# First projection of a hybrid encoder block: two value groups visited once for rows 2 to 8, the other four once for rows 4 to 8

## Chip, core and metric

The kernel runs on one NeuronCore of a Trainium2 chip. The metric is the device time of one execution in microseconds. The kernel before was run three times: 1234.67 us median, 1233.9 to 1236.42.

## The reference

One layer on 256 tokens of width 2048, all in float32. A modulation `mod = silu(c) @ w_ada + b_ada` gives six vectors of 2048 (shift, scale and gate, for each of two halves). Then:

```
h    = rms_norm(x, norm1_w) * (1 + scale1) + shift1
proj = h @ w_in                     # mq mk mv mo (gates) dq dk dv, 6152 columns
h_ml = mLSTM in chunks of 64 (conv and silu on mq, mk; values mv; output gate sigmoid(mo))
o_da = differential attention (q, k normed and rotated; two softmax maps a head; values dv)
x    = x + gate1 * (concat(h_ml, o_da) @ w_out)
h    = rms_norm(x, norm2_w) * (1 + scale2) + shift2
g, u = split(h @ w_gate_up)
x    = x + gate2 * ((silu(g) * u) @ w_down)
```

## The kernel before

**Products.** A float32 matrix product is made of three products of rounded parts: weights and activations are each split into a high part (ScalarE, `wh`, `hh`) and a low rest (VectorE, `wl`, `hl`), and TensorE adds high x high, high x low and low x high. One *step* (a "tick" in the code) is 256 rows of one group of 512 output columns: 12 matmuls of 128x512, two column halves of the activations' tokens, three products each. `weights_hi` and `weights_lo` split the weights up to two steps ahead of their use, four buffers of each. A *visit* is a run of steps of one output group that adds up in PSUM. When a visit ends, `project_done` copies the sum to `proj` (first visit of the group) or adds it there (VectorE, 128x1024).

**First projection.** `w_in` has twelve groups of 512 columns, each with eight steps (the list's rows 0 to 8, each 256 of the 2048 rows of the contraction). `EARLY` are two groups of q, two of k of the attention, and mq and mk; `LATE` are `DV` (two attention value groups), `MV` (two mLSTM value groups) and `MO` (two output gate groups). `SWEEPS` (line 52) lists in which order the groups are visited and for which rows. Sweep rows p0 to p1 need the transposed, modulated and split activations `h0_p0` to `h0_(p1-1)` (`make_hT`, line 447). The first 24 steps visit every group for row 0, then for row 1.

**Modulation.** The vectors of `w_ada` are made tile by tile (192 tiles of 512 KB), in the fixed order of `items` (line 300): for p = 0 to 7 four tiles of scale1 and four of shift1, then the 32 tiles of gate1, then scale2 and shift2, then gate2. The tiles of scale1 with p = 0, 1, 3, 4, 6, 7, of shift1 with p under 4 and of gate1 are multiplied on TensorE (`gv`, line 216 in the profile), the others on VectorE (line 185, `ada<-ada,silc`). `h0_p` needs the eight tiles of its p. The tiles share four buffers (`NADA`): the code issues a new tile's transfer when one has been used, on the SyncE queue, which also issues the weights' transfers (three buffers of 1 MB).

**Order of the work.** All engines' queues are written out by a plan in Python. For each step i the main loop (line 1338) splits weights, then calls `ada_use` until the number that `due(i)` names is reached, then runs works that are ready (`plan.run`; it holds them back while its account of VectorE's or ScalarE's backlog is over 2.3), then `ada_idle`, which uses a tile ahead of time if the plan takes it for landed and its engine for free, then forces whatever the step needs (`plan.until`), and then writes the 12 matmuls. Every engine works its queue in order. `due` (line 1249) comes from `ADA_PLAN` (line 1397): each entry (sweep, tiles, margin) spreads so many tiles evenly over the steps of that sweep, less the margin at its end, on top of 8:

```
a, b = spans[span]
loads.append((a, max(b - margin, a + 1), n))
...
n += k * min(max(i + 1 - a, 0), b - a) / (b - a)
```

**After the projection.** `prep` (norm, rotation, transposes of q, k), `conv`, `attend`, `attend_values`, `ml_scores`, `ml_values` and the rest are put between the steps as soon as the visits they need (`in{g}_8`) are done. The output projection starts at step 96 with the attention half.

Of the kernel before, what the change touches and what calls it, by code (L numbers as in the profile page):

```python
# [37 lines left out]
def on_pe(s, p):  # L38
# [9 lines left out]
DQ, DK, DV, MQ, MK, MV, MO = (0, 1), (2, 3), (4, 5), 6, 7, (8, 9), (10, 11)  # L48
EARLY = (DQ[0], DK[0], MQ, MK, DQ[1], DK[1])
LATE = (DV[0], DV[1], MV[0], MV[1], MO[0], MO[1])  # L50
FILL = 2
SWEEPS = (
    (EARLY + LATE, 0, 1), (EARLY + LATE, 1, 2), (EARLY + LATE, 2, 4), (LATE[6 - FILL:], 4, 6),
    (EARLY, 4, 8), (LATE[:6 - FILL], 4, 8), (LATE[6 - FILL:], 6, 8),
)
SQ0, SQ1 = True, False
FPAIRS = 6
# [107 lines left out]
def tile_block(ctx, tc, x, c, pos, par, w_ada, w_in, w_gt, w_out, w_gu, w_dn, out):  # L165
# [1076 lines left out]
    def load(span, n, margin):  # L1242
        a, b = spans[span]
        loads.append((a, max(b - margin, a + 1), n))

    for key, n, margin in ADA_PLAN:
        load(key, n, margin)
# [146 lines left out]
        return next(self.gen)  # L1394


ADA_PLAN = ((0, 12, 3), (1, 16, 4), (2, 24, 3), (3, 4, 0), (4, 8, 0), (5, 8, 0), ("wo", 16, 22), ("f0", 24, 5), ("f1", 32, 5), ("f2", 32, 8))


def _layout(a):  # L1400
# [68 lines left out]
```

## Time and profile before

| what | value |
|---|---|
| median of 3 runs | 1234.67 us |
| profiled execution, its own time | 1233.24 us |
| its span, first to last instruction | 1231.5 us |
| granted TensorE clock, mean | 0.992 |
| TensorE busy | 1208.9 us, 98% |
| VectorE busy | 815.3 us, 66% |
| ScalarE busy | 587.1 us, 48% |
| first projection, steps 0 to 95 | from 29.10 to 391.72 us |
| its third sweep, steps 24 to 47 | from 123.14 to 196.07 us |
| HBM traffic | 254 GB/s over the span |

In the profile, PE is TensorE, DVE VectorE, ACT ScalarE, POOL GpSimd, SPq the SyncE queue that issues transfers. Rows of the time line give start, duration, engine, line, operation, what is written and read, and how many were merged. Rows of waits give the engine and line that waited, what it waited for, and then total, number and longest. Rows of a window give its length, the busy time of each engine, the granted clock, the share of time that the DMA engines were busy, and GB/s. A matmul's busy time (0.39 us) overlaps the next one's: their starts are 0.227 us apart, so a step without other work takes 2.72 us.

### The profile page before, as it was taken

To read this page: it belongs to the slowest core of one execution; us is meant where nothing else is said; L and a number is where in the kernel's file an instruction comes from. 1 tells how busy PE (TensorE), PEld (TensorE's weight loads), DVE (VectorE), ACT (ScalarE), POOL (GpSimd) and SP (SyncE) were. 2 spreads that over 40 slices of the span, in tenths; PEclk is the share of its full clock that TensorE was granted. 3 is DMA by queue.
4 is the path that set the end of the run, shared out by engine and by line. 5 is a ranking of instruction groups with operands and counts; after the bars stand their busy time and mean duration, and the time that the engine had idled before them with its cause. 6 is when DMAs were issued, how large, how long until landed. Compare 5 with 4: busy or idle time off the path is not lost.

```text
span 1231.5 us, 15419 instructions
## 1 busy us (share of the span) xinstructions
PE 1208.9 (98%) x5842; PEld 956.2 (78%) x5842; DVE 815.3 (66%) x1064; ACT 587.1 (48%) x817; POOL 113.2 (9%) x250
## 2 busy tenths in 40 slices
PE   6999999999999999999999999999999999999998
PEld 2667878666778787788888888888888878888886
DVE  2656977577587998887988977445455454545443
ACT  3654454457566645855434544444444443343342
POOL 1010121210212412101100000000000000000000
PEclk8999999999999999999999999999999999999999
DMA  8879898757676898798999756555545545646471
GB/s 335 303 279 372 327 372 293 294 187 292 206 288 233 320 358 336 265 345 305 350 342 334 274 195 221 200 177 196 184 177 199 201 171 171 222 171 232 160 256 52
DMA packets 63260, 313.84 MB, mean 255 GB/s; under 512 B 6993, under 2 KB 7377, under 8 KB 41169
## 3 DMA queue, kind: packets, MB, share of 16 engines
q1 hardware_dynamic: 63186, 312.86, 70.1%
q8 instruction: 46, 0.75, 0.2%
q14 instruction: 28, 0.23, 0.1%
HBM read 310.73 MB, written 2.10 MB: 254 GB/s over the span
## 4 chain that ended last, share of the span: by engine, by line
PE 96%; DMA 1%; DVE 1%; ACT 1%; issue 0%; SPq 0%; POOL 0%; ACTq 0%
PE gv L216 3%; PE acc('dn', 0)_8036 L571 2%; PE acc('dn', 0)_8036 L569 2%; PE acc('dn', 2)_8838 L571 2%; PE acc('dn', 2)_8838 L570 2%; PE acc('dn', 1)_8458 L571 2%; PE acc('dn', 1)_8458 L570 2%; PE acc('dn', 0)_8036 L570 2%; PE acc('dn', 1)_8458 L569 2%; PE acc('dn', 2)_8838 L569 2%; DMA ada<-in_w_ada_dram 1%; PE apart('dn', 3)_9219 L571 1%; PE apart('dn', 3)_9219 L570 1%; PE acc('dn', 3)_9218 L571 1%; PE acc('dn', 3)_9218 L570 1%; PE apart('dn', 3)_9219 L569 1%
## 5 line engine op out<-in xcount | busy, mean ns | idle before, releaser
L181 DVE TENSOR_TENSOR wl<-r,wh 128x1024 fp32r<-128x1024 f32 x392 | 474.5, 1222 | 254.3 <-ACT wh L211 252.8
L211 ACT ACTIVATE wh<-r 128x1024 fp32r<-128x1024 f32 x392 | 410.3, 1058 | 409.6 <-DMA r<-in_w_gu_dram 62.1
L185 DVE SCALAR_TENSOR_TENSOR ada<-ada,silc 128x1024 f32<-128x1024 f32 x120 | 144.8, 1219 | 0.0
L377 POOL TENSOR_TENSOR modc<-part,gsum 128x2 f32<-128x2 f32 (+1 forms) x34 | 25.4, 747 | 395.1 <-DVE ada L185 277.5
L216 PE MATMUL gv<-ada,early 128*32 128x256 f32 x576 | 46.3, 416 | 4.3 <-DMA ada<-in_w_ada_dram 4.2
L216 PEld LDWEIGHTS gv<-ada,early 128*32 128x32 f32 x576 | 13.4, 112 | 29.4 <-issue 20.0
L569 PE MATMUL acc('dn', 0)_8036<-wh,aTh 128*128 128x512 f32 x88 | 35.9, 408 | 0.0
L379 POOL TENSOR_TENSOR modc<-modc,gsum 128x2 f32<-128x2 f32 (+1 forms) x58 | 30.9, 533 | 46.8 <-DVE ada L185 43.4
L571 PE MATMUL acc('dn', 0)_8036<-wh,aTl 128*128 128x512 f32 x88 | 34.3, 390 | 0.0
L570 PE MATMUL acc('dn', 0)_8036<-wl,aTh 128*128 128x512 f32 x88 | 34.3, 389 | 0.0
L569 PE MATMUL acc('dn', 1)_8458<-wh,aTh 128*128 128x512 f32 x88 | 34.2, 389 | 0.0
L570 PE MATMUL acc('dn', 1)_8458<-wl,aTh 128*128 128x512 f32 x88 | 34.2, 389 | 0.0
L571 PE MATMUL acc('dn', 1)_8458<-wh,aTl 128*128 128x512 f32 x88 | 34.2, 389 | 0.0
L569 PE MATMUL acc('dn', 2)_8838<-wh,aTh 128*128 128x512 f32 x88 | 34.2, 389 | 0.0
L570 PE MATMUL acc('dn', 2)_8838<-wl,aTh 128*128 128x512 f32 x88 | 34.2, 389 | 0.0
L571 PE MATMUL acc('dn', 2)_8838<-wh,aTl 128*128 128x512 f32 x88 | 34.2, 389 | 0.0
L181 DVE TENSOR_TENSOR hl<-hx,hh 128x512 fp32r<-128x512 f32 (+1 forms) x18 | 11.4, 632 | 26.5 <-ACT hh L211 26.2
L211 ACT ACTIVATE hx<-pt,modc,gcol 128x256 f32<-128x256 f32 (+1 forms) x36 | 17.4, 534 | 17.3 <-PE pt L220 11.5
L211 ACT ACTIVATE gr<-gv 128x256 f32<-128x256 f32 x18 | 6.9, 383 | 32.6 <-PE gv L216 32.6
L570 PEld LDWEIGHTS acc('dn', 0)_8036<-wl,aTh 128*128 128x128 f32 x88 | 16.5, 188 | 4.2 <-issue 1.0
L569 PEld LDWEIGHTS acc('dn', 0)_8036<-wh,aTh 128*128 128x128 f32 x88 | 16.5, 188 | 4.2 <-issue 1.0
L211 ACT ACTIVATE aTh<-at 128x512 fp32r<-128x512 f32 x22 | 11.9, 595 | 15.9 <-PE at L220 15.9
(987 smaller groups left out, 3019.0 us busy)
## 6 DMA issues: line engine op xcount, KB each, us to landing
ada<-in_w_ada_dram SPq DMA_DIRECT2D x192, 512.0 KB, 5.7
r<-in_w_gu_dram SPq DMA_DIRECT2D x76, 1024.0 KB, 5.0
r<-in_w_dn_dram SPq DMA_DIRECT2D x44, 1024.0 KB, 4.8
r<-in_w_in_dram SPq DMA_DIRECT2D x36, 1024.0 KB, 6.9
r<-in_w_out_dram SPq DMA_DIRECT2D x16, 1024.0 KB, 7.4
r<-in_w_in_dram SPq DMA_DIRECT2D x24, 512.0 KB, 5.9
r<-in_w_gu_dram SPq DMA_DIRECT2D x24, 512.0 KB, 5.3
x<-in_x_dram SPq DMA_DIRECT2D x4, 512.0 KB, 5.6
```

The costliest lines, as they stand in the source:

```text
L181: nc.vector.tensor_tensor(o, a, b, op=op)
L185: nc.vector.scalar_tensor_tensor(out=o, in0=a, scalar=s, in1=b, op0=op0, op1=op1, accum_out=accum)
L211: nc.scalar.activation(o, a, func, **kw)
L216: nc.tensor.matmul(o, l, r, start=start, stop=stop, **kw)
L377: nc.gpsimd.tensor_tensor(o, parts[0], parts[1], op=ALU.add)
L379: nc.gpsimd.tensor_tensor(o, o, y, op=ALU.add)
L569: nc.tensor.matmul(o, ah[:, s], wh[:, r], start=t["start"] and j == 0, stop=False)
L570: nc.tensor.matmul(o, ah[:, s], wl[:, r], start=False, stop=False)
L571: nc.tensor.matmul(o, al[:, s], wh[:, r], start=False, stop=t["stop"] and j == 1)
```

## The change

The third sweep (rows 2 to 4) leaves out the two attention value groups; `FIRST` = 2 names them. The extra visits of the two output gate groups (rows 4 to 6, ahead of the fourth sweep, and rows 6 to 8 at the end) are gone. The fourth sweep (q, k, mq, mk for rows 4 to 8) follows the third at once. After it the two attention value groups are visited once for rows 2 to 8, six steps each, and the other four late groups once for rows 4 to 8. There are 46 visits in place of 50, and 96 steps as before. Step 24 to 35 visit the same groups and rows in both. `ADA_PLAN` has its entries for the third to sixth sweep set anew: 28, 8, 4 and 4 tiles with no margin, in place of 24 (margin 3), 4, 8 and 8.

```
-FILL = 2
+FIRST = 2
 SWEEPS = (
-    (EARLY + LATE, 0, 1), (EARLY + LATE, 1, 2), (EARLY + LATE, 2, 4), (LATE[6 - FILL:], 4, 6),
-    (EARLY, 4, 8), (LATE[:6 - FILL], 4, 8), (LATE[6 - FILL:], 6, 8),
+    (EARLY + LATE, 0, 1), (EARLY + LATE, 1, 2), (EARLY + LATE[FIRST:], 2, 4), (EARLY, 4, 8),
+    (LATE[:FIRST], 2, 8), (LATE[FIRST:], 4, 8),
 )
...
-ADA_PLAN = ((0, 12, 3), (1, 16, 4), (2, 24, 3), (3, 4, 0), (4, 8, 0), (5, 8, 0), ("wo", 16, 22), ("f0", 24, 5), ("f1", 32, 5), ("f2", 32, 8))
+ADA_PLAN = ((0, 12, 3), (1, 16, 4), (2, 28, 0), (3, 8, 0), (4, 4, 0), (5, 4, 0), ("wo", 16, 22), ("f0", 24, 5), ("f1", 32, 5), ("f2", 32, 8))
```

## The prediction

> **What bounds the kernel now.** I read the page first (busy shares, then the 40 slices), then who waited for whom, then the third sweep of the first projection in windows and in order of time.
>
> ```profile
> span 1231.5 us, 15419 instructions
> ...
> PE 1208.9 (98%) x5842; PEld 956.2 (78%) x5842; DVE 815.3 (66%) x1064; ACT 587.1 (48%) x817; POOL 113.2 (9%) x250
> ...
> PE   6999999999999999999999999999999999999998
> ...
> DVE  2656977577587998887988977445455454545443
> ```
>
> TensorE is at work in every slice after the first, so no removed VectorE or ScalarE work shortens the span by itself. The time can only move by TensorE waits. Here are all that it has after 75 us:
>
> ```profile
> PE acc('gu', 0, 0)_4441 L569 <- ACT hh L211: 2.3, 2, 1.1
> PE acc('wo', 0)_3635 L571 <- DVE odl L185: 0.7, 1, 0.7
> PE pt L220 <- DVE hx L190: 0.7, 1, 0.7
> ```
>
> The reader is to see how little there is to win: only the 0.7 us at the start of the output projection lies behind the changed sweeps. The other two belong to the turn from output projection to feed-forward, which the change leaves alone. So the question is what the change may cost, and that is read from the third sweep (steps 24 to 47 before, 123.14 to 196.07 us):
>
> ```profile
> core 0: us, PE busy (x) PEld busy (x) DVE busy (x) ACT busy (x) POOL busy (x), PEclk, DMA share, GB/s
> 123.14:196.07 72.93, 72.93 (x369) 56.57 (x369) 61.37 (x70) 33.20 (x43) 14.38 (x22) 1.00 0.91 342
> 126.19:161.39 35.20, 35.20 (x178) 27.53 (x178) 35.06 (x43) 15.69 (x19) 8.17 (x10) 1.00 0.96 360
> 145.00:165.00 20.00, 20.00 (x112) 14.68 (x110) 16.58 (x20) 8.88 (x12) 3.49 (x4) 1.00 1.00 384
> ```
>
> For 35 us in it VectorE is as full as TensorE (35.06 of 35.20), and in part of that the DMA engines are full too (share 1.00 at 384 GB/s). TensorE does not wait there, but only just:
>
> ```profile
> 126.19 1.21 DVE L185 SCALAR_TENSOR_TENSOR ada<-ada,silc 128x1024 f32<-128x1024 f32 x1
> ...
> 127.33 1.21 DVE L185 SCALAR_TENSOR_TENSOR ada<-ada,silc 128x1024 f32<-128x1024 f32 x1
> ...
> 144.72 1.22 DVE L185 SCALAR_TENSOR_TENSOR ada<-ada,silc 128x1024 f32<-128x1024 f32 x1
> ...
> 149.28 1.22 DVE L181 TENSOR_TENSOR wl<-r,wh 128x1024 fp32r<-128x1024 f32 x1
> ```
>
> ```profile
> 148.13 0.39 PE L569 MATMUL acc('in', 1, 2)_1314<-wh,hh 128*128 128x512 f32 x1
> ...
> 150.85 0.39 PE L569 MATMUL acc('in', 3, 2)_1356<-wh,hh 128*128 128x512 f32 x1
> ```
>
> Step 33 starts at 148.13 and step 34 at 150.85, 2.72 us apart. Step 34's low weight half (wl) is ready at 149.28 + 1.22 = 150.50, 0.35 us ahead. VectorE's large operations follow each other in 127.33 - 126.19 = 1.14 us.
>
> **What the change removes.** Four visits, so four VectorE additions of an accumulator to proj, 4 x 1.14 = 4.6 us. They are hidden: the waits above hold none on proj. The count of matmuls (96 steps of 12), weight bytes and transfers (24 of 512 KB, 36 of 1024 KB) stay. I count 0.
>
> **What it moves.** The second half of the rows (h0_4 to h0_7) is now wanted from step 44, one group per step, so h0_7 by step 47 instead of 55. The plan therefore takes adaLN tiles 36 to 63 in 20 steps, 1.4 a step, where it took 24 in 21, 1.14 a step. I number tiles by their issue from 0: 44 to 47 and 52 to 55 go to VectorE, 48 to 51 and 56 to 59 to TensorE. By the plan's formula 48 and 49 are due at step 33 (now 35 and 36), 52 at 36 (38), 56 at 38 (42), 60 to 63 at 41 to 43 (48 to 51). The four ring buffers let a tile be issued only when the one four before it has been used.
>
> ```profile
> 145.97 0.33 SPq L316 DMA_DIRECT2D ada<-in_w_ada_dram  x1
> ```
>
> ```profile
> ada<-in_w_ada_dram SPq DMA_DIRECT2D x1, 512.0 KB, 5.0
> ```
>
> ```profile
> 153.67 0.64 PE L216 MATMUL gv<-ada,early 128*32 128x256 f32 x8
> ...
> 176.29 0.64 PE L216 MATMUL gv<-ada,early 128*32 128x256 f32 x8
> ```
>
> ```profile
> DMA to landing us min/median/max: 3.8/5.6/8.2
> ```
>
> **First new wait: tiles 48 and 49 at step 33.** Now tile 44's product starts at 144.72, tile 48 is issued at 145.97 when it is done, lands 5.0 us later (150.97) and is read at 153.67, 2.7 us to spare. After the change VectorE has 15 operations ahead of tile 44 from 126.19 on, not 16; at (144.72 - 126.19)/16 = 1.16 us it starts at 143.6 and ends at 144.7. Tile 45 is two operations on, ending at 147.0; tile 49 is issued then and with the median 5.6 us lands at 152.7. But TensorE comes to the pair in front of step 33, at about 148.1, and to tile 49 0.5 us later: it waits 152.7 - 148.6 = 4.1 us in all (2.3 with the shortest landing, 6.7 with the longest). Behind it on TensorE stand all matmuls of the sweep. The late wl halves (under 1 us by the same count) disappear under it. I take 4.0.
>
> **Second: tile 56 at step 38.** Now its predecessor 52 is due at step 38:
>
> ```profile
> 164.96 0.48 PE L569 MATMUL acc('in', 5, 2)_1476<-wh,hh 128*128 128x512 f32 x1
> ```
>
> ```profile
> 165.94 1.22 DVE L185 SCALAR_TENSOR_TENSOR ada<-ada,silc 128x1024 f32<-128x1024 f32 x1
> ```
>
> Its product ends at 167.16, 2.2 us after step 38 began, and only then can 56 be issued. After, 52 is due at 36 and 56 at 38, two steps or 5.44 us on. 2.2 + 5.6 - 5.44 = 2.4 us of wait; with 3.8 and 8.2 us, 0.6 and 5.0. I take 2.0, because a sweep that has just waited leaves the DMA engines less behind. Tiles 50, 51 and 57 to 63 come out with room by the same count.
>
> **The clock after a wait.** One long wait of this kind is in the trace, at step 9:
>
> ```profile
> PE gt L216 <- ACT hh L211: 2.3, 1, 2.3
> PE acc('in', 0, 0)_305 L570 <- DVE wl L181: 0.5, 1, 0.5
> PE gt L216 <- DVE hl L181: 0.4, 1, 0.4
> ```
>
> ```profile
> 64.90:67.50 2.60, 0.36 (x2) 0.00 (x0) 0.00 (x1) 2.54 (x5) 0.54 (x3) 1.00 0.98 384
> 68.00:71.40 3.40, 3.15 (x13) 1.97 (x17) 1.64 (x3) 0.27 (x1) 0.00 (x0) 0.64 0.75 252
> 72.50:79.00 6.50, 6.50 (x40) 4.37 (x38) 2.45 (x2) 2.84 (x4) 0.00 (x0) 1.00 0.70 236
> ```
>
> After 2.3 + 0.4 us of waiting the granted clock was 0.64 over 3.4 us, a loss of 0.36 x 3.4 = 1.2 us. The first new wait is longer than that, so I add 1.2; the second is shorter, 0 (both bounds: 0 to 1.2 each). [...] The trace's 2.7 us sufficed, and I go by it.
>
> **Small terms.** h0_7's transposes and splits come about a step before step 47 (the plan holds works back while VectorE's account is over 2.3): 0.4 us, from 0 to the 2.7 us that the forced one at step 9 cost. The value sums end 4 to 6 steps sooner, so odl is in time: -0.7 (0 to -1.0). TensorE's small matvecs cost less in pairs than alone:
>
> ```profile
> 214.88 1.07 PE L216 MATMUL gv<-ada,early 128*32 128x256 f32 x16
> 220.64 0.64 PE L216 MATMUL gv<-ada,early 128*32 128x256 f32 x8
> ```
>
> 2 x 0.64 - 1.07 = 0.2 us for each pair; 50 and 51, a pair now, come apart: 0.3, and up to 1.5 either way for the 32 tiles of the gate, which the plan puts where it finds room.
>
> **Sum**: 4.0 + 2.0 + 1.2 + 0.4 - 0.7 + 0.3 = +7.2 us on the profiled execution's own 1233.24 (span 1231.5 and 1.7 around it): 1240.4, or 1240.5. That execution lies 1.4 us under the median of the runs (1234.67), inside or just under their 1233.9 to 1236.42; against the median it is +0.5%. Within 0.2%, or 2.5 us, no change could be told.
>
> **Rivals.** (a) *The transfers are in time.* With landings near 3.8 us the waits are 2.3 and 0.6, the clock holds, h0_7 is free and the start of the output projection gives 0.7: +2.2 us, and with luck in pairing +0.7: 1234 to 1236, no change. For it: over 160 to 170 us the queue already served more than the 384 quoted, and landings vary twofold. Against: the shortest landing is not the usual one while the engines are full.
> (b) *Faster.* The place is the start of the output projection: attention and cells done 4 to 6 steps earlier give back 0.7 to 1.0 us, and gate tiles in pairs 1.5; it decides if tiles 48, 49 and 56 are there when asked for, that is, if the landing is under some 2 us for 49. -2.5: 1230.7. Against: no landing under 3.8 us in that stretch.
> (c) *DMA becomes the bound of the whole sweep.* 20 weight halves and 28 tiles are 48 x 0.524 = 25.2 MB; at 384 GB/s 65.5 us, where TensorE needs 20 x 2.72 + 7.6 (72.93 - 24 x 2.72, its small work) = 62.0. 3.5 us of that, the two waits at 4.1 and 2.4, both with 1.2 of clock, and a forced h0_7 (2.7): +15, 1248. For it: 25.2 MB in 62 us is 406 GB/s. Against: six weight steps lie in the buffers when the sweep starts.
> (d) *The change doesn't do what it says*: if the plan's idle rule took tiles ahead of the due count, rates would stay; but it did so for two of 24 only. In (a).
>
> **Chances.** Forecast 0.53, (a) 0.25, (b) 0.08, (c) 0.14. The forecast's own range is 1237 to 1245.5. For 8 of 10 I leave out most of (b) and the far end of (c): 1233 to 1247.5. Faster by over 0.2%: 0.08, (b). Within: 0.25, (a). Slower: 0.67.
>
> **What would show it.** Idle time of TensorE in front of gv at steps 33 and 38, put down to the ada transfer, 4 and 2 us, right if there, wrong if gv follows its matmul without a gap. A granted clock under 1 for about 3.4 us after the first. No odl wait at the output projection. VectorE full from 126 to 150 us and 4 fewer proj additions. The prediction is wrong if the third sweep has no TensorE wait: then the time is that of (a) or (b).

## The result, and the profile after

The changed kernel takes 1249.18 us (median of 4 runs, 1247.71 to 1250.11); the kernel before, beside it, 1234.29 (4 runs, 1233.35 to 1236.42). The ratio is 1.0118, with a 95% interval of 1.0106 to 1.0130. The change makes the kernel 14.9 us slower. The prediction had the sign and half of the size.

The page of the changed kernel, profiled in an execution of 1248.64 us:

```profile
span 1246.9 us, 15415 instructions
...
PE 1214.1 (97%) x5842; PEld 957.1 (77%) x5842; DVE 810.9 (65%) x1060; ACT 586.0 (47%) x817; POOL 105.4 (8%) x250
```

TensorE has the same 5842 instructions, VectorE 4 fewer and 4.4 us less work (815.3 to 810.9): the four additions are gone, and the time rose all the same. So waits or the clock of TensorE must hold the loss. All waits of TensorE after 75 us (engine, line, what it waited for; total, times, longest):

```profile
PE gv L216 <- DMA ada<-in_w_ada_dram: 4.2, 3, 2.3
PE pt L220 <- DVE hx L190: 2.7, 1, 2.7
PE acc('gu', 0, 0)_4433 L569 <- ACT hh L211: 2.1, 2, 1.1
PE acc('in', 0, 4)_1662 L569 <- ACT hh L211: 1.8, 1, 1.8
PE at L220 <- DVE fp L181: 1.8, 2, 1.4
PE ot L220 <- ACT ml L211: 0.7, 1, 0.7
PE acc('gu', 1, 5)_5856 L570 <- DVE wl L181: 0.4, 1, 0.4
```

Seven groups where there were three, 13.7 us in place of 3.7. The first, fourth and sixth lie in the first projection; the second, third, fifth and seventh lie in stages that the change doesn't touch. To see how much time each place took, I read the start of the first matmul of a step from the order of time, in both traces. The difference in length of each stretch, after less before (and the same for three experiments below):

| steps | before, us | changed kernel | before, tiles at the new rate | changed, slower tiles | changed, old places | changed, both |
|---|---|---|---|---|---|---|
| up to 0 | 29.10 | +0.37 | +0.67 | +0.39 | +0.54 | +0.67 |
| 0 to 24 | 94.04 | -0.76 | -0.41 | +0.47 | -0.47 | -0.72 |
| 24 to 33 | 24.99 | +4.43 | +4.65 | 0.00 | +3.87 | 0.00 |
| 33 to 38 | 16.83 | +0.62 | +0.85 | 0.00 | +0.88 | +0.17 |
| 38 to 48 | 31.11 | +7.06 | +3.50 | +7.74 | +7.02 | +8.92 |
| 48 to 104 | 225.80 | -4.10 | +7.85 | -3.65 | -4.13 | -3.66 |
| 104 to 126 | 59.84 | 0.00 | +4.47 | 0.00 | 0.00 | 0.00 |
| 126 to 130 (the turn) | 15.58 | +4.47 | +2.79 | +0.03 | +1.57 | +0.01 |
| 130 to 188 | 160.84 | -0.01 | -0.04 | +0.99 | 0.00 | -0.01 |
| 188 to 224 (end of gate and up) | 102.61 | +3.33 | +0.25 | +3.03 | +0.62 | +0.06 |
| 224 to the end | 470.79 | -0.02 | -0.01 | -0.02 | -0.01 | +0.03 |

(48 to 104 gives time back because the transposes for `h0_7` and the small products behind them, which stood at steps 52 and 53, now stand at steps 46 and 47.) Not every microsecond of a profile is the edit's: two runs below are the kernel before, unchanged up to step 104, and they reach that step 1.17 and 1.00 us later than it. Up to step 104 the sum is +7.6 us, beside the predicted +7.2. Another 7.8 us comes later: 4.5 at the turn from output projection to feed-forward, 3.3 in the last feed-forward sweep of gate and up. These the prediction did not see.

The third sweep of the changed kernel in the order of time (start, duration, and in brackets the idle time ahead and what ended it):

```profile
150.36 0.64 PE L216 MATMUL gv<-ada,early 128*32 128x256 f32 x8 [2.26 <-DMA ada<-in_w_ada_dram]
151.61 0.64 PE L216 MATMUL gv<-ada,early 128*32 128x256 f32 x8 [0.61 <-DMA ada<-in_w_ada_dram]
...
169.05 0.64 PE L216 MATMUL gv<-ada,early 128*32 128x256 f32 x8 [1.38 <-DMA ada<-in_w_ada_dram]
...
201.68 0.50 PE L569 MATMUL acc('in', 0, 4)_1662<-wh,hh 128*128 128x512 f32 x1 [1.83 <-ACT hh L211]
```

Tiles 48 and 49 are waited for in front of step 33, tile 56 in front of step 38, and `h0_7`, forced late, in front of step 47. The SyncE queue shows tile 48's issue, and then 56's:

```profile
144.13 3.75 SPq L316 DMA_DIRECT2D ada<-in_w_ada_dram  x3
...
164.67 3.76 SPq L316 DMA_DIRECT2D ada<-in_w_ada_dram  x3
```

From 144.13 to the use at 150.36 are 6.2 us, from 164.67 to 169.05 4.4 us: TensorE stands idle for what is left of these two landings.

The turn, first in the kernel before and then in the changed one:

```profile
487.97 0.70 PE L220 MATMUL pt<-ident,hx 128*128 128x128 f32 x4 [0.65 <-DVE hx L190]
489.81 0.50 PE L569 MATMUL acc('gu', 0, 0)_4441<-wh,hh 128*128 128x512 f32 x1 [1.15 <-ACT hh L211]
```

```profile
497.67 1.11 PE L220 MATMUL pt<-ident,hx 128*128 128x128 f32 x4 [2.73 <-DVE hx L190]
499.76 0.80 PE L569 MATMUL acc('gu', 0, 0)_4433<-wh,hh 128*128 128x512 f32 x1 [0.98 <-ACT hh L211]
```

The transposes wait 2.1 us longer, and the matmul behind them takes 0.80 us in place of 0.50: the granted clock is 0.50 from 497.66 to 504.49 us. ScalarE ahead of it in the changed kernel:

```profile
475.73 0.63 ACT L211 ACTIVATE junk<-x2r 128x512 bf16<-128x512 f32 x1 [4.18 <-DVE x2r L181]
...
490.97 2.01 ACT L211 ACTIVATE wh<-r 128x1024 fp32r<-128x1024 f32 x2 [5.81 <-DMA r<-in_w_gu_dram]
```

And the issue of the first feed-forward weights, before and after:

```profile
471.52 0.33 SPq L515 DMA_DIRECT2D r<-in_w_gu_dram  x1
```

```profile
478.00 4.43 SPq L316 DMA_DIRECT2D ada<-in_w_ada_dram  x2
482.52 1.11 SPq L515 DMA_DIRECT2D r<-in_w_gu_dram  x1
```

A shift by the 7.6 us so far would give 479.1; it is issued 3.4 us later than that, behind two tile issues in the same queue (478.00 + 4.43), which wait for VectorE's products. ScalarE's high halves then wait 5.81 us for these weights.

### The profile page after: what moved, and what is told of

Its sections match the earlier page's. It is cut to its first block, busy times and chain, and to the rows that moved or that the text cites. A ratio compares the mean times of both kernels' runs of the same rounds, so it can differ in the third digit from the quotient of the medians.

```text
span 1246.9 us, 15415 instructions
## 1 busy us (share of the span) xinstructions
PE 1214.1 (97%) x5842; PEld 957.1 (77%) x5842; DVE 810.9 (65%) x1060; ACT 586.0 (47%) x817; POOL 105.4 (8%) x250
## 4 chain that ended last, share of the span: by engine, by line
PE 85%; DVE 7%; DMA 3%; issue 2%; ACT 2%; POOL 0%; SPq 0%; DVEq 0%; ACTq 0%
PE gv L216 3%; DVE wl L181 2%; DVE ada L185 2%; DMA ada<-in_w_ada_dram 2%; PE acc('dn', 0)_8028 L571 2%; PE acc('dn', 0)_8028 L569 2%; PE acc('dn', 2)_8830 L571 2%; PE acc('dn', 2)_8830 L570 2%; PE acc('dn', 1)_8450 L571 2%; PE acc('dn', 1)_8450 L570 2%; PE acc('dn', 0)_8028 L570 2%; PE acc('dn', 2)_8830 L569 2%; PE acc('dn', 1)_8450 L569 2%; DMA r<-in_w_gu_dram 1%; ACT wh L211 1%
## 5 line engine op out<-in xcount | busy, mean ns | idle before, releaser
L569 PE MATMUL acc('dn', 0)_8028<-wh,aTh 128*128 128x512 f32 x88 | 35.9, 408 | 0.0
L571 PE MATMUL acc('dn', 0)_8028<-wh,aTl 128*128 128x512 f32 x88 | 34.3, 390 | 0.0
L570 PE MATMUL acc('dn', 0)_8028<-wl,aTh 128*128 128x512 f32 x88 | 34.3, 389 | 0.0
L569 PE MATMUL acc('dn', 1)_8450<-wh,aTh 128*128 128x512 f32 x88 | 34.2, 389 | 0.0
L570 PE MATMUL acc('dn', 1)_8450<-wl,aTh 128*128 128x512 f32 x88 | 34.2, 389 | 0.0
L571 PE MATMUL acc('dn', 1)_8450<-wh,aTl 128*128 128x512 f32 x88 | 34.2, 389 | 0.0
L569 PE MATMUL acc('dn', 2)_8830<-wh,aTh 128*128 128x512 f32 x88 | 34.2, 389 | 0.0
L570 PE MATMUL acc('dn', 2)_8830<-wl,aTh 128*128 128x512 f32 x88 | 34.2, 389 | 0.0
L571 PE MATMUL acc('dn', 2)_8830<-wh,aTl 128*128 128x512 f32 x88 | 34.2, 389 | 0.0
L570 PEld LDWEIGHTS acc('dn', 0)_8028<-wl,aTh 128*128 128x128 f32 x88 | 16.5, 188 | 4.2 <-issue 1.0
```

Of the source, the lines that this page charges most:

```text
L569: nc.tensor.matmul(o, ah[:, s], wh[:, r], start=t["start"] and j == 0, stop=False)
L570: nc.tensor.matmul(o, ah[:, s], wl[:, r], start=False, stop=False)
L571: nc.tensor.matmul(o, al[:, s], wh[:, r], start=False, stop=t["stop"] and j == 1)
```

## The experiments

Two questions: is the early loss the rate at which the tiles are wanted (theory), or the new visits (rival)? And what makes the late loss: the order of work at the turn, or the places at which tiles are multiplied after the first projection, which have moved although `due` asks for the same there?

**The changed kernel with ScalarE's squares later.** In the changed kernel the squares of the third output block stand one half step sooner in ScalarE's queue than before, so that it stands 4.18 us for `x2r` with the weights' halves behind. This holds them back.

```
         def squares():
             yield 0
+            if g == 2:
+                yield 0
+                yield 0
             for t in range(2):
                 square_x(1, g, t)
```

> The changed kernel, with one edit: the sums of squares of the third output block (x2_2) are put into ScalarE's queue two half steps later, behind one more high weight half, as in the kernel before. Theory (the turn is late because these squares, which wait 4.2 us for the residual, stand in ScalarE's queue ahead of the weights' high halves, and the low halves and the next weights' transfers behind them): the 2.7 us wait at the turn falls to about 0.7, no half clock after it, the time from step 126 to step 152 comes back from 82.0 to 77.5 us, so 4.5 us less than the changed kernel: about 1244. Rival (the DMA engines are behind at the turn because of the adaLN tiles): the wait stays, 1249.

Measured: 1248.11 us (1245.41 to 1249.06), ratio 1.0106 (1.0090 to 1.0121). Its waits have this line at the turn, and a window there (its length, busy time and count of TensorE, its weight loads, VectorE, ScalarE, GpSimd, granted clock, DMA share, GB/s):

```profile
PE pt L220 <- DVE hx L190: 0.7, 1, 0.7
```

```profile
499.10:502.50 3.40, 3.40 (x9) 2.54 (x8) 2.49 (x6) 1.30 (x3) 0.00 (x0) 0.50 0.00 0
```

The median, expected near 1244, cannot be told from the changed kernel's. In the profiled execution, the lowest of the four, the wait is back to what it was before, and so are the two waits behind it. At the turn 1.6 of 4.5 us stay, all of it half clock, and the last gate and up sweep still loses 2.2.

**The kernel before with the squares sooner.**

```
+        if i == turning - 8:
+            plan.run(force=True, only={"x2_2"})
...
+            if i == turning - 8:
+                plan.run(force=True, only={"sqrt"})
```

> The kernel before, with the same squares and the square root's table load put one high weight half sooner into ScalarE's queue, as the changed kernel has them; nothing else. Theory: the turn loses what it lost in the changed kernel, a wait of some 2.7 us in place of 0.7 and half clock for some us, 3 to 5 us in all: 1237 to 1239. Rival (DMA behind at the turn because of the tiles' places): no change, 1234.

Measured: 1234.84 us (10 runs, 1233.61 to 1236.92), ratio 1.0006 (0.9996 to 1.0015). The same order costs nothing here: the wait at the turn stays at 0.65 us. The squares' place alone is not the cause, so the theory fell as it stood; what part of it holds is told behind the run with the changed kernel's places.

**The kernel before with the tiles at the new rate.** The visits are the old ones; only the plan asks for 28 tiles in the 20 steps after step 24.

```
-ADA_PLAN = ((0, 12, 3), (1, 16, 4), (2, 24, 3), (3, 4, 0), (4, 8, 0), (5, 8, 0), ...
+ADA_PLAN = ((0, 12, 3), (1, 16, 4), (2, 28, 4), (3, 0, 0), (4, 8, 0), (5, 8, 0), ...
```

> The kernel before, with its sweeps as they were, but the plan of adaLN tiles for the third sweep that of the changed kernel: 28 tiles over 20 steps in place of 24 over 21 (none in the sweep behind it). Theory (the tile rate alone makes the waits): TensorE waits for the ada transfer before steps 33 and 38, about 2.9 and 1.4 us as in the changed kernel, and for no h0 group; +4.3 us: 1238 to 1239, plus what moved tiles do at the turn. Rival (the order of the sweeps makes them): no wait there, 1234.

Measured: 1259.03 us (1254.43 to 1260.59), ratio 1.0191 (1.0169 to 1.0214). Its third sweep in the order of time:

```profile
151.22 0.64 PE L216 MATMUL gv<-ada,early 128*32 128x256 f32 x8 [2.48 <-DMA ada<-in_w_ada_dram]
152.48 0.64 PE L216 MATMUL gv<-ada,early 128*32 128x256 f32 x8 [0.62 <-DMA ada<-in_w_ada_dram]
...
170.16 0.64 PE L216 MATMUL gv<-ada,early 128*32 128x256 f32 x8 [1.61 <-DMA ada<-in_w_ada_dram]
```

The same three waits stand at the same places with almost the same lengths, without the new visits. So the rate makes them. The time is 20 us above the forecast, and the rest of the loss is this kernel's own: 7.25 us of wait for `o` where the output projection begins, and, from within that wait on, a granted clock of 0.50 (over 406.60 to 416.80 us). Why `o` is so late there stays open.

**The changed kernel with the tiles earlier**, in the second sweep, where VectorE is less full (in the changed kernel 28.97 of 43.75 us there, 66.15 of 85.04 in steps 24 to 47).

```
-... (1, 16, 4), (2, 28, 0), (3, 8, 0), ...
+... (1, 20, 2), (2, 24, 0), (3, 8, 0), ...
```

> The changed kernel, with four of the third sweep's 28 tiles taken in the second sweep (20 tiles over 10 steps there, then 24 over 20 steps, 1.2 a step in place of 1.4). Theory: tiles 48 and 56 are then due over three steps after 44 and 52, so the waits for ada before steps 33 and 38 fall from 2.9 and 1.4 us to under 1 in sum; the second sweep, whose VectorE is at 65%, takes the tiles without a wait; the 1.8 us wait for h0_7 stays: 1245, if the later stages stay as they were. Rival (DMA engines are the bound of the sweep): the waits only move into the second sweep, 1249.

Measured: 1247.73 us (1245.93 to 1248.17), ratio 1.0103 (1.0086 to 1.0120). In the order of time:

```profile
122.31 0.47 PE L569 MATMUL acc('in', 11, 1)_1091<-wh,hh 128*128 128x512 f32 x1 [1.59 <-DVE proj L181]
...
130.29 0.50 PE L569 MATMUL acc('in', 0, 2)_1114<-wh,hh 128*128 128x512 f32 x1 [1.83 <-ACT hh L211]
...
149.62 0.64 PE L216 MATMUL gv<-ada,early 128*32 128x256 f32 x8 [0.83 <-DMA ada<-in_w_ada_dram]
```

The waits at steps 33, 38 and 47 are gone, and one of 0.83 us stands at step 30. But the queues fill earlier: TensorE now waits for an accumulator's addition in the second sweep, and at step 25 for a forced `h0` group, with 3.41 us of half clock behind that (0.50 over 132.05 to 135.46 us). Up to step 104 the loss is 8.6 us in place of 7.6. The wait has moved, not gone.

**The changed kernel with the old places.** From step 97 on, a table makes each tile be used in the half step in which the kernel before used it.

```
+        if i >= FROM:
+            take(2 * i)
...
+FROM = 97
+PLACES = (169, 170, 173, 178, 181, 186, 186, 188, 190, 195, ...
```

> The changed kernel, with one edit: from step 97 on the adaLN tiles are multiplied in the very half steps in which the kernel before does it (a table of places in place of the due counts and the idle rule). Theory (the 7.8 us lost behind step 104 come from the tiles' places among the weights' splits and transfers, and from nothing that the changed sweeps do there): steps 104 to the end take what they take in the kernel before, so no 2.7 us wait at the turn, no wait at the last feed-forward sweep, and the +7.6 us up to step 104 stay: 1241 to 1242. Rival (the loss behind step 104 is another effect of the new sweeps): it stays, 1247 to 1249.

Measured: 1243.44 us (1242.84 to 1247.49), ratio 1.0078 (1.0059 to 1.0096). Of its waits, the one at the turn:

```profile
PE pt L220 <- DVE hx L190: 0.7, 1, 0.7
```

The third sweep is as in the changed kernel, and the two late losses fall from 4.47 and 3.33 us to 1.57 and 0.62. So the places of tiles make most of the late loss. The 1.57 at the turn is clock alone (0.50 over 498.35 to 501.77 us); it is taken up in the last section.

**The kernel before with the changed kernel's places** from step 104 on (the same `take`, with at most one tile in a half step).

> The kernel before, with the tiles from step 104 on multiplied in the half steps in which the changed kernel does it (at most one a half step until it has caught up). Theory: the sweeps up to step 104 stay as they were and the waits behind them appear, 2 to 3 us at the turn with half clock after it and 1.5 to 3.3 us in the last feed-forward sweep: 1239 to 1242. Rival: no change, 1234.5.

Measured: 1240.07 us (1238.58 to 1242.16), ratio 1.0045 (1.0029 to 1.0060). Its waits:

```profile
PE at L220 <- DVE fp L181: 1.7, 2, 1.4
PE acc('wo', 1)_3790 L576 <- DVE wl L181: 1.1, 1, 1.1
...
PE pt L220 <- DVE hx L190: 0.7, 1, 0.7
```

The last gate and up sweep loses 4.1 us, with the changed kernel's wait of `at` for `fp` (1.4 us). The places alone make that loss, and some of their own where low halves come late (1.1 us at step 110, and a like one after the turn). The turn's wait did not come. The traces show why, in the time from the issue of the first feed-forward weights to the start of step 126:

| run | issue | step 126 starts | us ahead | wait of `pt` at the turn, us |
|---|---|---|---|---|
| kernel before | 471.52 | 481.71 | 10.19 | 0.65 |
| kernel before, squares sooner | 474.52 | 482.89 | 8.37 | 0.65 |
| kernel before, changed kernel's places | 475.92 | 484.19 | 8.26 | 0.65 |
| changed kernel, squares later | 481.34 | 489.97 | 8.63 | 0.65 |
| changed kernel | 482.52 | 489.33 | 6.81 | 2.73 |
| changed kernel, old places | 479.24 | 489.43 | 10.19 | 0.65 |

```profile
474.52 0.33 SPq L515 DMA_DIRECT2D r<-in_w_gu_dram  x1
```

```profile
481.34 0.38 SPq L515 DMA_DIRECT2D r<-in_w_gu_dram  x1
```

(These are the second and the fourth run.) The squares alone put the issue back by 1.8 us, the places alone by 1.9, and either costs no wait. The changed kernel has both, 3.4 us, and waits. With the old places its squares too stand where they stood before. The two other profiled runs with 6.8 us (the new rate, the earlier tiles) wait 1.7 and 2.4 us; all others wait 0.65 to 0.73. So the turn's wait takes both parts.

**The changed kernel with slower tiles in the third sweep**, five of the 28 left to the fourth.

```
-... (2, 28, 0), (3, 8, 0), ...
+... (2, 23, 0), (3, 13, 0), ...
```

> The changed kernel, with 23 tiles in the third sweep's 20 steps (1.15 a step, the rate of the kernel before) and 13 in the fourth sweep. Theory (the rate makes the waits before steps 33 and 38): those go, but tiles 59 to 63 are then not done by step 47, which needs h0_7, and the plan forces them there: a wait of 5 to 10 us in front of steps 46 and 47, with half clock; about as slow as the changed kernel in all, 1245 to 1252. Rival (the waits are the DMA engines' and not the rate's): waits before steps 33 and 38 stay beside it.

Measured: 1243.27 us (1242.27 to 1245.66), ratio 1.0076 (1.0059 to 1.0092). Steps 24 to 38 are as long as before, to the last digit; what is left comes in one piece ahead of step 47, where the last tiles for `h0_7` are forced:

```profile
197.99 0.64 PE L216 MATMUL gv<-ada,early 128*32 128x256 f32 x8 [3.24 <-DMA ada<-in_w_ada_dram]
```

A slower rate moves the wait to the due date. It costs less than was expected, 3.24 us with a granted clock of 1.00 over 193.08 to 199.91 us, and less in all (+4.95 us by step 104, not +7.6), but the date itself, 64 tiles by step 47, costs. The turn changes as well, +0.03 us in place of +4.47, though nothing was edited behind step 67: the stages behind follow the tiles of the first projection.

**Both edits at once**: slower tiles, and the old places from step 97.

> The changed kernel with both single edits at once: tiles of the third sweep at 23 instead of 28 a sweep (the rest in the fourth), and the places of the tiles from step 97 on as in the kernel before. If the two causes (tiles wanted too soon in the third sweep; tile places behind step 104) stand side by side and add up: the slower tiles left +4.95 us by step 104 and the places left 0 to 2.2 us behind it, so 1239.2 to 1241.5, ratio 1.004 to 1.006. If they are one cause seen twice, the gains do not add: about 1243, ratio 1.007. If the places cost something new with the other plan: over 1244.

Measured: 1239.59 us (5 runs, 1238.75 to 1240.04), ratio 1.0039 (1.0025 to 1.0054), inside the 1239.2 to 1241.5 that two separate causes give. All its waits after 75 us:

```profile
PE gv L216 <- DMA ada<-in_w_ada_dram: 2.7, 1, 2.7
PE acc('gu', 0, 0)_4433 L574 <- ACT hh L211: 2.3, 2, 1.1
PE aT L220 <- ACT pm L211: 1.2, 1, 1.2
PE pt L220 <- DVE hx L190: 0.7, 1, 0.7
PE acc('in', 0, 4)_1642 L574 <- ACT hh L211: 0.5, 1, 0.5
```

From step 104 on every stretch is within 0.06 us of the kernel before. With the old places the whole late loss is gone. The causes stand side by side: the date in the first projection, and the places of tiles behind it.

**Two more tiles in the second sweep**, with the old places, to take the rest.

```
-... (1, 16, 4), (2, 28, 0), (3, 8, 0), ...
+... (1, 18, 3), (2, 23, 0), (3, 11, 0), ...
```

> As the run above, but two more of the tiles are taken in the second sweep (18 at two a step, margin 3), and 23 in the third. Theory (what is left is a shortage of places for 64 tiles before step 47): the wait for a late tile at steps 46 and 47 shrinks from 3.2 us by the two tiles' worth, near 1 us, with no wait in the second sweep, since its rate stays two a step: 1237 to 1239, still slower than before by 0.2 to 0.4%. Rival: the second sweep has no room either (20 tiles in twelve steps cost a forced group of h0 and a half-clock stretch there): a new wait of 1.5 to 2 us near 120 to 130 us and no gain, 1240 to 1243.

Measured: 1248.07 us (1246.26 to 1248.95), ratio 1.0105 (1.0090 to 1.0120). The rival came, and dearer than written. In the order of time (its added code shifts the line numbers by 5):

```profile
128.86 0.50 PE L576 MATMUL acc('in', 0, 2)_1116<-wh,hl 128*128 128x512 f32 x1 [1.29 <-DVE hl L181]
153.49 0.64 PE L216 MATMUL gv<-ada,early 128*32 128x256 f32 x8 [1.60 <-DMA ada<-in_w_ada_dram]
...
202.52 0.50 PE L574 MATMUL acc('in', 0, 4)_1653<-wh,hh 128*128 128x512 f32 x1 [1.83 <-ACT hh L211]
```

The second sweep has no room for two more tiles either, and the waits of the third come back as well. Steps 48 to 104 give nothing back here (-0.04 us), with another wait of 2.06 us for `ot` at step 78, whose cause stays open. No kernel tried here beats the one before; a deeper ring of tile buffers was not tried.

## Why the prediction was wrong

Point by point, in its own steps:

- **What the change removes**: right. Four additions and 4.4 us of VectorE went, and no time with them.
- **First new wait, tiles 48 and 49 at step 33**: right in place, cause and bounds, 2.26 + 0.61 = 2.9 us where 4.0 were taken. The product ahead of tile 48 started at 142.9, not 143.6, so 48 was issued at 144.13, and 49 too was sooner than the sum had it.
- **Second, tile 56 at step 38**: right, 1.4 us for 2.0.
- **The clock after a wait**: wrong. After the wait at step 33 the clock stayed at 1.00 (149.50 to 155.70 us); why it did is not shown. It fell at the turn instead, to 0.50 for 6.8 us. The size was misread too: the 0.64 over 3.40 us mixes half and full clock, and the stretch behind step 9 is 3.41 us at 0.50, a loss of 1.7 us and not 1.2.
- **Small terms**: `h0_7` was forced after all, 1.83 us for 0.4 (its bounds were 0 to 2.7). The `odl` wait went, as forecast, but `ot` waits 0.7 us for `ml` at step 89, so the -0.7 bought nothing. The small matvecs cannot be summed apart from the rest.
- **Sum**: +7.2 predicted, +7.6 measured at step 104. The agreement is partly luck. The waits come to 6.3 (2.9, 1.4, 1.83, 0.7, small ones 0.2, less the `odl` wait); the rest is net of a later start (+0.37), a half-clock stretch at step 9 that the profile of before has and that of the changed kernel has not, small work that moved, and the 1 us or so by which unchanged code differs. It is not split here.
- **The step that failed** stands in the first part: the waits at the turn "belong to the turn from output projection to feed-forward, which the change leaves alone". The sum had no term behind the first projection. It should have had one of 7.8 us in this execution. The plan that writes the queues takes tiles ahead of time by its accounts of the engines, and these differ after another first projection: tile 112 is used at step 100 in place of 103, tile 128 at step 121 in place of 122. On VectorE and in the SyncE queue those tiles stand between the weights' halves. At the turn the two issues ahead of the first feed-forward weights are such tiles, and ScalarE's squares have moved too. That the places make the loss is shown by three runs: old places take most of it away alone, and all of it with both edits (0.01 and 0.06 us left); new places in the old kernel bring the loss of the last gate and up sweep (4.1 us). That the tiles of the first projection move the stages behind it is shown by the slower tiles. That the accounts do it is read from the code, not shown by a run: `due` asks for 80 tiles by the start of the output projection in both kernels, and by the two tables of places 105 are used by then before and 110 after, so `ada_idle` has taken the rest.
- **Rivals**: (a) and (b) needed the transfers in time, and they were not. (c), 1248 us, is nearest in number but not in mechanism: it wanted two waits of 4.1 and 2.4 us, a clock loss at each and the DMA engines as the bound of the whole sweep. What brought the time near it is the turn and the last gate and up sweep. (d) is out: the changed plan did raise the rate.

## What to carry to other kernels

Where queues are written by a plan with accounts, an edit in one stage can move work in all later ones; ask what is placed by those accounts behind the edit, and give the sum a term for it, or pin the later places before judging the edit. Here a due date that was brought forward cost at the date or ahead of it: a lower or an earlier rate moved the wait from step 33 to 47, or to steps 22 to 25, and never took it away. And a wait of TensorE can cost more than its length: behind the 2.73 us at the turn of the changed kernel stand 6.8 us at a granted clock of 0.50.

## What the runs showed of the hardware

I had taken one clock drop behind the wait at step 9 as a rule: 2.7 us of waiting, then a slower clock. The same wait in the changed kernel, 2.26 and 0.43 us, is followed by no drop at all. From 34.79 to 1229.45 us the kernel before has one drop, 3.41 us at a granted clock of 0.50, behind step 9; from 36.87 to 1245.10 us the changed kernel has one, 6.83 us at 0.50, at the turn. The drops and the 3.41 us (the length of the shorter one) ahead of each, and in the changed kernel two stretches of that length at step 9 and two at step 33, a whole number of lengths ahead of its drop (columns as above):

```profile
65.51:68.92 3.41, 0.96 (x6) 0.68 (x7) 1.42 (x2) 1.93 (x4) 0.06 (x1) 1.00 1.02 414
68.92:72.34 3.42, 3.42 (x15) 1.68 (x14) 0.72 (x2) 1.21 (x2) 0.00 (x0) 0.50 0.66 212
```

```profile
64.17:67.58 3.41, 2.18 (x10) 1.46 (x8) 1.59 (x3) 2.57 (x4) 2.25 (x6) 1.00 0.99 393
67.58:70.99 3.41, 1.95 (x10) 1.35 (x10) 2.15 (x3) 0.94 (x2) 0.00 (x0) 1.00 0.91 365
146.09:149.50 3.41, 2.01 (x9) 1.31 (x7) 3.41 (x6) 0.65 (x2) 1.12 (x1) 1.00 0.96 346
149.50:152.91 3.41, 1.94 (x19) 0.96 (x20) 3.41 (x5) 0.52 (x1) 1.83 (x1) 1.00 1.00 363
494.25:497.66 3.41, 0.69 (x4) 0.22 (x2) 2.19 (x7) 1.02 (x3) 0.00 (x0) 1.00 0.96 369
497.66:501.08 3.42, 2.44 (x7) 1.84 (x8) 2.74 (x7) 2.34 (x6) 0.00 (x0) 0.50 0.28 108
501.08:504.49 3.41, 3.41 (x9) 2.64 (x9) 2.30 (x6) 1.24 (x2) 0.00 (x0) 0.50 0.01 5
```

Ahead of the two drops TensorE was busy for 0.96 and 0.69 of 3.41 us. In the changed kernel the waits at steps 9 and 33 are each split over two stretches, busy for 1.94 to 2.18 us, and the clock stayed at 1.00. At the turn the first 3.42 us at 0.50, 2.44 us of them busy, were followed by 3.41 more, and these, busy throughout, by 1.00 (504.50 to 1245.10 us). At step 47 it was likewise: with the slower tiles the wait of 3.24 us lies in stretches of 1.67 and 1.92 us busy, and the clock was 1.00 in both; with both edits the one of 2.71 us lies in a stretch of 0.64 us busy, and the next, 197.58 to 200.99, ran at 0.50. The changed kernel with the old places has half clock at the turn, where the kernel before, with the same waits (0.65, 1.15, 1.13 us), was at 1.00 (485.35 to 492.18 us, busy for 2.67 and 2.37 of 3.41):

```profile
494.94:498.35 3.41, 1.61 (x9) 1.01 (x9) 2.91 (x7) 2.17 (x7) 0.00 (x0) 1.00 0.91 384
498.35:501.77 3.42, 3.42 (x10) 2.64 (x9) 2.70 (x8) 1.51 (x3) 0.00 (x0) 0.50 0.04 14
```

So the length of a wait did not tell what it cost: 2.26 and 0.43 or 0.44 us at step 9 were followed by 0.50 in the kernel before (68.92 to 72.34 us), and by 1.00 in the changed kernel (68.70 to 72.10) and with both edits (69.40 to 73.00). What decides it is not shown, nor a limit of the busy time: 1.76 us (earlier tiles, 128.64 to 132.05) were followed by half clock, 1.67 (slower tiles, 193.08 to 196.49) were not.

Where it comes, 3.41 us at 0.50 in work that is otherwise full cost 3.41 x 0.50 = 1.7 us, an estimate from these rows. So two profiles can differ by that much at one place where their waits are alike: the 1.57 us at the turn with the old places is of this kind, since with both edits the waits are the same to 0.01 us, the clock is 1.00 (491.12 to 501.36 us) and the stretch is 0.01 us from the kernel before. So is the 1.6 us with the squares later (0.50 over 499.10 to 502.50 us).
